# Hybrid gMLP and dilated-attention trunk: ScalarE and VectorE of the attention held to program order, softening one half slot behind the scores, output weights asked for earlier

## The chip, the cores and the metric

The kernel runs on one core of a Trainium2 chip. The metric is device time in microseconds. Engines are named as in the profile: PE (TensorE), DVE (VectorE), ACT (ScalarE), POOL (GpSimd), and SP, which issues most DMAs.

## The reference

Two layers, each a token mixer and a squared-ReLU MLP, with adaLN modulation and a DeepNorm residual; S = 1024, D = 1024. Layer 0 mixes with a chunked causal gMLP, layer 1 with causal dilated attention: three patterns of 16 heads, E = 64, merged by their log-sum-exp.

```python
for g, (window, dilation) in enumerate(B_PATTERNS):    # (128, 1), (512, 4), (2048, 16)
    o, lse = dilated_branch(qkv[:, :, g, 0], qkv[:, :, g, 1], qkv[:, :, g, 2], window, dilation, slopes)
    outs.append(o)
    lses.append(lse)
wts = jax.nn.softmax(jnp.stack(lses, axis=0), axis=0)[..., None]
o = jnp.sum(wts * jnp.stack(outs, axis=0), axis=0)
return o.reshape(B, S, B_HEADS * B_HEAD_DIM) @ w_out
```

## The kernel before

Every fp32 operand is cut into two halves, hi and lo, so that a product is three matmuls (hi hi, hi lo, lo hi). `split` (L100) does it: ACT casts hi (L102), DVE subtracts to lo (L103).

The stages run one after another: adaLN vectors, mixer of layer 0, MLP, the values of layer 1 (`values`, psv on PE; their halves qs are stored by POOL, L1270), the attention (`attention`, L1348), its output projection, the last MLP. The change is in the attention.

The attention works through 24 groups: eight pairs of heads (hp), and for each the patterns g = 2, 1, 0. A group has eight slots of two halves, so a pair has 48 half slots. Functions are hung into half slots with a rank, `in_half(half_slot, rank)` or `at(slot, half)`, and a loop calls those of each half slot in the order of their ranks. These steps make up a group:

- `scores` (rank 1): for two heads, PE multiplies queries and keys into sc, one PSUM bank a head, two in all.
- `soften` (rank 3): DVE adds the bias and takes the minimum (L1551, a custom operation and the reading of its accumulator, stat), ACT takes the exponential and its sum (L1553).
- `transposes` (rank 0) and `halve` (rank 2): PE transposes the probabilities into pT, a split makes pThi and pTlo.
- `weighted` (rank 0, PE, pv L1611), `gather` (ACT copies pv into oT, L1619) and `join` (DVE adds a later part to it, L1623).

Between them `project` streams the projections of queries and keys of later groups (psq and psk, L1434, 512 columns each). Its weights are loaded by SP and cut to wqk_hi and wqk_lo; five units of eight steps run before the first slot.

The three patterns of a pair are merged while the next pair runs (`merge`). `read` loads the minima and sums (mst); `factors` works out three weights per head (mm, ma L1683 to 1687, the exponential L1688 on ACT, mal and ma again L1690 to 1695) and stores them to w_dram (SP, L1697); `spread` loads each back as a row for all partitions (bc, L1704); twelve steps scale (L1716) and add (L1720) and cut the result. The merges of the seventh and eighth pair end in oTs, the operand of the output projection. `load_unit` (L1764) loads that projection's weights (wo) into the buffers that projection weights and others leave; `accumulate` multiplies (psoa, psob L1794), and ACT copies out the first sums (acc, L1803).

The Python order is not the order of the instructions: the tile framework's scheduler puts each engine's instructions in an order of its own. `tc.keep_in_program_order(ins)` pins an instruction behind the one that was issued ahead of it on its engine. Before, only some steps of the merge are pinned.

## Time and profile before

| | us |
|---|---|
| median of three runs | 2736.19 |
| lowest, highest | 2726.71, 2740.26 |
| the profiled execution | 2735.97 |
| its span | 2734.3 |
| attention, first psq to last sc | 1455.8 to 2019.5 |
| mean granted clock of PE | 0.992 |

A row of a timeline has the start, the duration, the engine, the line, the operation, the written and read tiles (buffer numbers left out), the shapes, and in brackets how long the engine had been idle and what it waited for. Matmul rows overlap: the next one's start tells the pace. A row of waits has the engine, its instruction, the releaser, and the total, the number and the longest of such waits.

### The profile page before, as it was taken

To read this page: it belongs to the slowest core of one execution; us is meant where nothing else is said; L and a number is where in the kernel's file an instruction comes from. 1 tells how busy PE (TensorE), PEld (TensorE's weight loads), DVE (VectorE), ACT (ScalarE), POOL (GpSimd) and SP (SyncE) were. 2 spreads that over 40 slices of the span, in tenths; PEclk is the share of its full clock that TensorE was granted. 3 is DMA by queue.
4 is the path that set the end of the run, shared out by engine and by line. 5 is a ranking of instruction groups with operands and counts; after the bars stand their busy time and mean duration, and the time that the engine had idled before them with its cause. 6 is when DMAs were issued, how large, how long until landed. Compare 5 with 4: busy or idle time off the path is not lost.

```text
span 2734.3 us, 37203 instructions
## 1 busy us (share of the span) xinstructions
PE 2653.9 (97%) x13194; PEld 2190.8 (80%) x13194; DVE 2019.3 (74%) x3652; ACT 1389.6 (51%) x2621; POOL 129.9 (5%) x211
## 2 busy tenths in 40 slices
PE   6999999999999999999999999999999999999998
PEld 5788888887888878888888878888777888878886
DVE  6787698787888878666664677777657966577887
ACT  3354375555443454434344666666655755554332
POOL 1000000000000001111111000000010000000000
PEclk9999999999999999999999999999999999999999
DMA  7534337667967656665646555666883554485562
GB/s 263 155 119 135 116 137 225 228 221 255 336 217 257 225 179 214 235 218 204 227 157 194 140 151 157 168 169 175 245 197 112 192 197 153 150 312 193 169 208 85
DMA packets 342223, 525.76 MB, mean 192 GB/s; under 512 B 52572, under 2 KB 169732, under 8 KB 342036
## 3 DMA queue, kind: packets, MB, share of 16 engines
q1 hardware_dynamic: 323060, 455.21, 52.7%
q0 software_dynamic: 18976, 68.17, 6.8%
q8 instruction: 103, 1.69, 0.3%
q14 instruction: 84, 0.69, 0.1%
HBM read 376.93 MB, written 146.36 MB: 191 GB/s over the span
## 4 chain that ended last, share of the span: by engine, by line
PE 61%; DVE 15%; issue 11%; DMA 7%; ACT 5%; SPq 1%; POOL 1%; DVEq 0%; POOLq 0%; ACTq 0%
PE psv L1323 15%; PE psd L957 12%; PE psua L798 7%; PE psk L1434 5%; PE psuc L798 3%; PE psd_wout L389 3%; DMA adaw<-in_ada_w_dram 3%; PE psu L368 3%; PE pv L1611 2%; PE psv L470 2%; ACT p L1553 2%; PE sc L1532 2%; PE psq L1434 2%; DVE adaacc L128 1%; PE psub L798 1%
## 5 line engine op out<-in xcount | busy, mean ns | idle before, releaser
L798 PE MATMUL psua<-right,left 128*128 128x512 f32 x1536 | 363.2, 390 | 0.1
L957 PE MATMUL psd<-rhi,lhi 128*128 128x512 f32 x896 | 349.9, 390 | 3.0 <-ACT part L829 3.0
L957 PE MATMUL psd<-rlo,lhi 128*128 128x512 f32 x896 | 349.4, 390 | 0.2
L957 PE MATMUL psd<-rhi,llo 128*128 128x512 f32 x896 | 349.3, 390 | 0.0
L798 PEld LDWEIGHTS psua<-right,left 128*128 128x128 f32 x1536 | 287.2, 188 | 61.1 <-DVE right L103 1.2
L1553 ACT ACTIVATE p<-p,stat 128x128 f32<-128x128 f32 (+1 forms) x384 | 168.4, 440 | 110.0 <-DVE stat L1551 108.9
L957 PEld LDWEIGHTS psd<-rhi,lhi 128*128 128x128 f32 x896 | 168.6, 188 | 39.0 <-ACT part L829 3.9
L957 PEld LDWEIGHTS psd<-rlo,lhi 128*128 128x128 f32 x896 | 168.7, 188 | 36.0 <-DVE rlo L103 1.1
L957 PEld LDWEIGHTS psd<-rhi,llo 128*128 128x128 f32 x896 | 168.5, 188 | 34.9
L798 PE MATMUL psuc<-right,left 128*128 128x512 f32 x768 | 187.2, 390 | 0.0
L128 DVE SCALAR_TENSOR_TENSOR adaacc<-adaw,silu_c,adaacc 128x512 f32<-128x512 f32 x168 | 128.6, 775 | 55.2 <-DMA adaw<-in_ada_w_dram 54.4
L798 PEld LDWEIGHTS psuc<-right,left 128*128 128x128 f32 x768 | 143.6, 188 | 29.9 <-DVE right L103 0.2
L103 DVE TENSOR_TENSOR pTlo<-pT,pThi 128x512 fp32r<-128x512 f32 (+1 forms) x160 | 98.7, 621 | 63.3 <-ACT pThi L102 62.3
L103 DVE TENSOR_TENSOR left<-ws,left 128x512 fp32r<-128x512 f32 x128 | 87.9, 688 | 74.0 <-ACT left L102 72.2
L103 DVE TENSOR_TENSOR llo<-lraw,lhi 128x1024 fp32r<-128x1024 f32 x112 | 136.4, 1218 | 1.5 <-ACT lhi L102 1.5
L1434 PE MATMUL psk<-form_L,wqk_hi 128*128 128x512 f32 x384 | 131.3, 423 | 0.0
L102 ACT CAST left<-ws 128x512 fp32r<-128x512 f32 x128 | 79.1, 620 | 99.3 <-DVE ws L719 89.5
L102 ACT CAST lhi<-lraw 128x1024 fp32r<-128x1024 f32 x112 | 117.3, 1047 | 9.7 <-PE psd L957 3.3
L1323 PE MATMUL psv<-vrhi,form_S 128*128 128x512 f32 x384 | 120.1, 391 | 1.1 <-DVE vpart L1263 0.6
L1323 PE MATMUL psv<-form_S,vrhi 128*128 128x512 f32 x384 | 118.2, 389 | 0.0
L1551 DVE CUSTOM_DVE_ANT_0 p<-sc,bias 128x128 f32<-128x128 f32 (+1 forms) x384 | 110.4, 346 | 3.5 <-PE sc L1532 3.2
L102 ACT CAST rhi<-rraw 128x1024 fp32r<-128x1024 f32 x48 | 50.5, 1053 | 118.2 <-issue 80.1
(335 smaller groups left out, 6161.4 us busy)
## 6 DMA issues: line engine op xcount, KB each, us to landing
lraw<-forms SPq DMA_DIRECT2D x112, 512.0 KB
adaw<-in_ada_w_dram SPq DMA_DIRECT2D x192, 256.0 KB
up<-in_mlp_w_up_dram SPq DMA_DIRECT2D x64, 512.0 KB
forms<-s SPq DMA_DIRECT2D x128, 256.0 KB
rraw<-in_mlp_w_down_dram SPq DMA_DIRECT2D x64, 512.0 KB
vraw<-in_b_w_qkv_dram SPq DMA_DIRECT2D x50, 512.0 KB
forms<-part SPq DMA_DIRECT2D x96, 256.0 KB
v<-vs POOLq DMA_DIRECT2D x48, 512.0 KB, 4.4
```

What stands on the lines that cost most here:

```text
L102: first = A.copy(hi, src) if hi_engine is A else hi_engine.tensor_copy(hi, src)
L103: return first, lo_engine.tensor_tensor(lo, src, hi, op=ALU.subtract)
L128: ins = V.scalar_tensor_tensor(acc[:], raw[:], silu_c[:, k : k + 1], acc[:], ALU.mult, ALU.add)
L368: T.matmul(dst, s[a], m[b], start=(n == 0), stop=(n == last))
L389: T.matmul(p[:], stat[a][:, k, o : o + P], u[b][:, w], start=n == 0, stop=n == count - 1)
L470: T.matmul(sums[u, half][:], units[u][a_][:, k * P : (k + 1) * P], hT[half][b_][:, k, :], start=k == 0 and a_ + b_ == 0, stop=k == KD - 1 ...
L798: T.matmul(acc, w[:, a, k, :], right[p][:, b, k, :], start=p in (1, 2, 5) and k + a + b == 0, stop=k == 3 and a == 1, skip_group_check=True)
L957: ins = T.matmul(sums[kind, m][:], l[a][:, k, m * P : (m + 1) * P], r[b][:, k, :], start=p in (1, 5, 2, 3) and kp + k + a + b == 0, stop=k ...
L1323: T.matmul(acc, rows[:, m * P : (m + 1) * P], cols_, start=p in (1, 2, 5) and kp + k + a + b == 0, stop=kp == 1 and k == 1 and a == 1, ski ...
L1434: T.matmul(p[:], wu[a][:, k * P : (k + 1) * P], h_op(k, half, b), start=k + c_ == 0, stop=k == KD - 1 and c_ == 2)
L1551: V.tensor_tensor_reduce(out=pr, in0=banks[e][:, sl], in1=st["bias"][:, width - w :], scale=-0.125, scalar=3e38, op0=ALU.add, op1=ALU.min, ...
L1553: A.activation(pr, pr, AF.Exp, bias=nm, scale=-1.0, accum_out=l)
```

## The change

From the lead of the projections to the last slot, every instruction of DVE and ACT is pinned to program order, so that the order in which the loop calls the functions is the order on these two engines; PE, POOL and SP are left to the scheduler. The single pins in the merge go. The half slots are set anew for this: the minimum and the exponential of a score are called one half slot later, as two functions (rank 2.2 and 3); the subtraction of pTlo is a function of its own (rank 2.4), behind the cast of pThi (2) and the joins (2.3); the split of a projection is left to the end of its half slot; the merge's factors come in two parts, a slot and a half apart, and its scaling and adding have other half slots; the last group's scores start in the half slots of the others. Output weights are asked for earlier in program order. The set of instructions is the same on every engine.

```diff
@@ -38,7 +38,22 @@
-    V, A, G, T = nc.vector, nc.scalar, nc.gpsimd, nc.tensor
+    in_order = [False]
+    class Ordered:
+        def __init__(self, engine):
+            self.engine = engine
+        def __getattr__(self, name):
+            call = getattr(self.engine, name)
+            def traced(*a, **k):
+                ins = call(*a, **k)
+                return tc.keep_in_program_order(ins) if in_order[0] else ins
+            return traced
+    V, A, G, T = Ordered(nc.vector), Ordered(nc.scalar), nc.gpsimd, nc.tensor
@@ -1396,6 +1411,12 @@
             def h_op(k, half, part):
...
+            late = []
+            def leave():
+                while late:
+                    late.pop(0)()
@@ -1435,7 +1456,7 @@
-                            split(hi, lo, by_pos(p[:], g))
+                            late.append(lambda hi=hi, lo=lo, p=p, g=g: split(hi, lo, by_pos(p[:], g)))
@@ -1481,7 +1502,7 @@
-                starts = {0: (0, 4, 6, 10) if last_one else (0, 4, 8, 11), 1: (0, 4, 10), 2: (0, 8)}[g]
+                starts = {0: (0, 4, 8, 11), 1: (0, 4, 10), 2: (0, 8)}[g]
@@ -1537,26 +1558,33 @@
                 def soften(m, part):
...
-                    for t, w, sl in spans[part : part + 1]:
-                        for e, st in enumerate(heads):
-                            if w == P and st.get("half") is not None:
-                                pr = st.pop("half")[:, P : 2 * P]
-                            else:
-                                whole = ql.tile([P, 2 * P], F32, name=f"p_{2 * hp + e}_{g}_{t}", tag="p", bufs=16)
-                                pr = whole[:, 0:w]
-                                if w == P and g:
-                                    st["half"] = whole
-                            col = (t % 2) * 4 + t // 2 if g == 1 else t
-                            nm, l = stat[:, 0, e, col : col + 1], stat[:, 1, e, col : col + 1]
-                            V.tensor_tensor_reduce(out=pr, in0=banks[e][:, sl], in1=st["bias"][:, width - w :], scale=-0.125,
-                                                   scalar=3e38, op0=ALU.add, op1=ALU.min, accum_out=nm)
-                            A.activation(pr, pr, AF.Exp, bias=nm, scale=-1.0, accum_out=l)
-                            st["probs"][t] = pr
+                    t, w, sl = spans[part]
+                    for e, st in enumerate(heads):
+                        if w == P and st.get("half") is not None:
+                            pr = st.pop("half")[:, P : 2 * P]
+                        else:
+                            whole = ql.tile([P, 2 * P], F32, name=f"p_{2 * hp + e}_{g}_{t}", tag="p", bufs=16)
+                            pr = whole[:, 0:w]
+                            if w == P and g:
+                                st["half"] = whole
+                        col = (t % 2) * 4 + t // 2 if g == 1 else t
+                        V.tensor_tensor_reduce(out=pr, in0=banks[e][:, sl], in1=st["bias"][:, width - w :], scale=-0.125,
+                                               scalar=3e38, op0=ALU.add, op1=ALU.min, accum_out=stat[:, 0, e, col : col + 1])
+                        st["probs"][t] = pr
+                def exponentials(m, part):
+                    stat = my["stat"]
+                    t, _, _ = my["spans", m][1][part]
+                    col = (t % 2) * 4 + t // 2 if g == 1 else t
+                    for e, st in enumerate(heads):
+                        pr = st["probs"][t]
+                        A.activation(pr, pr, AF.Exp, bias=stat[:, 0, e, col : col + 1], scale=-1.0, accum_out=stat[:, 1, e, col : col + 1])
...
-                        in_half(2 * base + slot + part, 3)(lambda m=m, part=part: soften(m, part))
+                        in_half(2 * base + slot + part + 1, 2.2)(lambda m=m, part=part: soften(m, part))
+                        in_half(2 * base + slot + part + 1, 3)(lambda m=m, part=part: exponentials(m, part))
@@ -1592,7 +1620,12 @@
-                        split(hi[:, 0:end], lo[:, 0:end], pst[:, 0:end])
+                        A.copy(hi[:, 0:end], pst[:, 0:end])
+                        pT[m] = (hi, lo, pst, end)
+                    def low(m, pT=pT):
+                        hi, lo, pst, end = pT[m]
+                        V.tensor_tensor(lo[:, 0:end], pst[:, 0:end], hi[:, 0:end], op=ALU.subtract)
@@ -1631,6 +1664,7 @@
+                        in_half(half_slot, 2.4)(lambda m=m, f=low: f(m))
@@ -1639,7 +1673,7 @@
-                                in_half(when_added, 2)(lambda b=b, f=join: f(b))
+                                in_half(when_added, 2.3)(lambda b=b, f=join: f(b))
@@ -1664,10 +1698,6 @@
-                def in_order(ins):
-                    if hp < N_PAIRS - 1:
-                        tc.keep_in_program_order(ins)
@@ -1675,17 +1705,22 @@
-                @at(*((base + 5, 1) if hp < N_PAIRS - 1 else (base + 1, 1)))
+                @at(*((base + 5, 0) if hp < N_PAIRS - 1 else (base + 1, 1)))
                 def factors():
...
-                    nm, l = st[:, :, 0, :], st[:, :, 1, :]
+                    nm = st[:, :, 0, :]
...
-                    tc.keep_in_program_order(V.tensor_tensor(m[:], nm[:, 0], nm[:, 1], op=ALU.min))
+                    V.tensor_tensor(m[:], nm[:, 0], nm[:, 1], op=ALU.min)
...
+                    box["m"] = a
+                @at(*((base + 6, 1) if hp < N_PAIRS - 1 else (base + 1, 1)))
+                def weights():
+                    l, a = box["st"][:, :, 1, :], box["m"]
@@ -1696,7 +1731,7 @@
-                @at(*((base + 6, 0) if hp < N_PAIRS - 1 else (base + 1, 1)))
+                @at(*((base + 6, 1) if hp < N_PAIRS - 1 else (base + 1, 1)))
@@ -1713,11 +1748,11 @@
-                    in_order(V.tensor_tensor(bc, o, bc, op=ALU.mult))
+                    V.tensor_tensor(bc, o, bc, op=ALU.mult)
...
                 def add(g, half):
...
-                    in_order(V.tensor_tensor(box[0][:, w], box[0][:, w], box[g][:, w], op=ALU.add))
+                    V.tensor_tensor(box[0][:, w], box[0][:, w], box[g][:, w], op=ALU.add)
@@ -1725,7 +1760,7 @@
-                    in_order(split(hi, lo, box[0][:, w])[1])
+                    split(hi, lo, box[0][:, w])
@@ -1736,7 +1771,7 @@
-                    in_half(2 * base + ((23, 25, 29, 31, 35, 37, 39, 41, 43, 45, 47, 51)[n] if hp < N_PAIRS - 2 else n + 22), 4)(f)
+                    in_half(2 * base + ((23, 25, 29, 31, 35, 36, 39, 40, 43, 47, 49, 53)[n] if hp < N_PAIRS - 2 else n + 22), 4)(f)
@@ -1763,7 +1798,7 @@
-            for k, half_slot in ((3, -34), (0, -32), (1, -30), (2, -27), (4, -15), (7, 11), (5, 17), (6, 18)):
+            for k, half_slot in ((0, -64), (1, -56), (3, -48), (2, -38), (4, -33), (7, 11), (5, 17), (6, 18)):
@@ -1832,13 +1867,16 @@
+            in_order[0] = True
...
+                leave()
...
+                    leave()
@@ -1848,7 +1886,8 @@
-            assert next(stream, None) is None
+            assert next(stream, None) is None and not late
+            in_order[0] = False
```

Below, rows of the built programs. In the rows of after every instruction of DVE and ACT has line 51, that of the wrapper. ACT where the values end and the attention begins (qs: high halves of value sums; wqk_hi: of projection weights), before:

```order
L102 CAST wqk_hi<-wq_2_raw 128x1024
L102 CAST wqk_hi<-wk_2_raw 128x1024
L102 CAST qs_1_4_3_11892<-psv_0_1_3_11491 128x512
L102 CAST qs_1_3_0_11909<-vpart_1_6_0_11685 128x512
L102 CAST qs_1_3_1_11926<-vpart_1_6_1_11703 128x512
L102 CAST qs_1_3_2_11943<-vpart_1_6_2_11724 128x512
L102 CAST wqk_hi<-wk_1_raw 128x1024
L102 CAST wqk_hi<-wq_2_raw 128x1024
L102 CAST qs_1_3_3_11960<-vpart_1_6_3_11742 128x512
```

and after:

```order
L51 CAST qs_1_4_3_11892<-psv_0_1_3_11491 128x512
L51 CAST qs_1_3_0_11909<-vpart_1_6_0_11685 128x512
L51 CAST qs_1_3_1_11926<-vpart_1_6_1_11703 128x512
L51 CAST qs_1_3_2_11943<-vpart_1_6_2_11724 128x512
L51 CAST qs_1_3_3_11960<-vpart_1_6_3_11742 128x512
L51 CAST wqk_hi<-wq_2_raw 128x1024
L51 CAST wqk_hi<-wk_2_raw 128x1024
L51 CAST qhi_2_12029<-psq_2_1_12031 128x16x32
L51 CAST qhi_2_12029<-psq_2_0_12058 128x16x32
```

The cuts of the first two projection weights stood ahead of the last five value splits and now stand behind them all.

DVE in the fourth pair's merge (ISA p: softens and their accumulators; mm, ma, mal: factors), before:

```order
L1551 ISA stat_2_15608 128x1
L1683 TENSOR_TENSOR mm_15840<-mst_15705 128x16
L1684 TENSOR_TENSOR mm_15840<-mm_15840,mst_15705 128x16
L1687 TENSOR_TENSOR ma_15843<-mm_15840,mst_15705 128x16 x3
L1690 TENSOR_TENSOR mal_15848<-ma_15843,mst_15705 128x48
L1691 TENSOR_TENSOR mal_15848<-mal_15848 128x16
L1692 TENSOR_TENSOR mal_15848<-mal_15848 128x16
L1623 TENSOR_TENSOR oT_0_15660<-oT_0_15660,pv_0_1_15751 64x512
L1693 RECIPROCAL mal_15848<-mal_15848 128x16
L1695 TENSOR_TENSOR ma_15843<-ma_15843,mal_15848 128x16 x3
L103 TENSOR_TENSOR pTlo_2_0_15868<-pT_2_0_15862,pThi_2_0_15867 128x512
L103 TENSOR_TENSOR qlo_2_15762<-psq_2_1_15763,qhi_2_15761 128x16x32
```

and after:

```order
L51 ISA stat_2_15606 128x1
L51 ISA p_2_6_15838,stat_2_15606<-sc_2_1_15771,bias_2_15607 128x128
L51 ISA stat_2_15606 128x1
L51 ISA p_2_6_15840,stat_2_15606<-sc_2_1_15772,bias_2_15609 128x128
L51 ISA stat_2_15606 128x1
L51 TENSOR_TENSOR pTlo_2_0_15853<-pT_2_0_15847,pThi_2_0_15852 128x512
L51 TENSOR_TENSOR mal_15864<-ma_15826,mst_15697 128x48
L51 TENSOR_TENSOR mal_15864<-mal_15864 128x16 x2
L51 RECIPROCAL mal_15864<-mal_15864 128x16
L51 TENSOR_TENSOR ma_15826<-ma_15826,mal_15864 128x16 x3
L51 TENSOR_TENSOR oT_0_15652<-oT_0_15652,pv_0_1_15749 64x512
```

pTlo of the next group stood behind all the factors and a join; now mm and the first ma are issued ahead of these softens, and pTlo stands right behind the softens, ahead of mal, the reciprocal, the last ma and the join.

DVE in the last merge but one, where bc is scaled for the first time, before:

```order
L1623 TENSOR_TENSOR oT_2_18588<-oT_2_18588,pv_2_1_18629 64x512
L103 TENSOR_TENSOR pTlo_2_0_18666<-pT_2_0_18646,pThi_2_0_18665 128x512
L1716 TENSOR_TENSOR bc_2_18512<-oT_2_17726,bc_2_18512 128x512
L1551 ISA p_1_3_18669,stat_1_18553<-sc_1_1_18651,bias_1_18554 128x256
L1551 ISA stat_1_18553 128x1
L1551 ISA p_1_3_18672,stat_1_18553<-sc_1_1_18652,bias_1_18556 128x256
L1551 ISA stat_1_18553 128x1
```

and after:

```order
L51 ISA p_1_3_18672,stat_1_18557<-sc_1_1_18652,bias_1_18560 128x256
L51 ISA stat_1_18557 128x1
L51 ISA p_1_5_18684,stat_1_18557<-sc_1_1_18651,bias_1_18558 128x256
L51 ISA stat_1_18557 128x1
L51 ISA p_1_5_18686,stat_1_18557<-sc_1_1_18652,bias_1_18560 128x256
L51 ISA stat_1_18557 128x1
L51 TENSOR_TENSOR oT_2_18586<-oT_2_18586,pv_2_1_18625 64x512
L51 TENSOR_TENSOR bc_2_18517<-oT_2_17724,bc_2_18517 128x512 x2
L51 TENSOR_TENSOR pTlo_2_1_18722<-pT_2_1_18716,pThi_2_1_18721 128x512
```

The first scale stood ahead of four softens, and now both of its halves stand behind them and a join, with the next pTlo behind the scale.

## The prediction

> **What bounds the kernel now.** I read the page first, then its busy time in stretches of 100 us, then what PE waited for inside the attention, and last the rows around each of those waits. The page names the engine.
>
> ```profile
> span 2734.3 us, 37203 instructions
> PE 2653.9 (97%) x13194; PEld 2190.8 (80%) x13194; DVE 2019.3 (74%) x3652; ACT 1389.6 (51%) x2621; POOL 129.9 (5%) x211
> ```
>
> PE is busy for 97% of the span, so a reordering on DVE and ACT pays only where PE stands still. The profiled execution took 2735.97 us, 1.7 us more than its span and 0.2 us less than the median of 2736.19 us, so one sum serves for both. Two of the attention's stretches; the columns are the stretch, its length, then the busy share of PE, PEld, DVE, ACT and POOL, and PE's clock.
>
> ```profile
> 1800.00:1900.00 100.00, 98.50 (x708) 83.17 (x707) 78.64 (x251) 69.77 (x215) 4.03 (x9) 1.00 0.61 173
> 1900.00:2000.00 100.00, 92.06 (x635) 77.01 (x634) 69.28 (x224) 61.23 (x195) 6.79 (x12) 0.97 0.82 234
> ```
>
> PE idles 1.5 and 8 us in these 100, and DVE (69 and 79%) and ACT (61 and 70%) have room. Between 1450 and 2040 us these are all of PE's waits: total, times, longest.
>
> ```profile
> PE pv L1611 <- DVE pTlo L103: 11.6, 19, 1.3
> PE psoa L1794 <- ACT acc L1803: 6.4, 1, 6.4
> PE pv L1611 <- ACT pThi L102: 1.8, 5, 0.6
> PE sc L1532 <- DMA bk<-qk: 0.5, 1, 0.5
> PE pv L1611 <- DVE oT L1623: 0.2, 1, 0.2
> ```
>
> They sum to 20.5 us. Idle time can also lower the clock: here stretches of 10 us with their clock, and PE after two waits.
>
> ```profile
> 1560.00:1570.00 10.00, 8.77 (x51) 6.99 (x50) 5.81 (x20) 4.72 (x16) 0.34 (x1) 0.83 0.65 172
> 1580.00:1590.00 10.00, 8.62 (x52) 6.85 (x51) 7.43 (x20) 6.80 (x21) 1.63 (x2) 0.83 0.56 176
> 1630.00:1640.00 10.00, 8.77 (x47) 6.97 (x47) 6.24 (x29) 6.03 (x22) 0.83 (x2) 0.84 0.61 172
> 1700.00:1710.00 10.00, 8.76 (x61) 7.16 (x60) 6.97 (x32) 6.07 (x23) 0.78 (x2) 1.00 0.54 148
> 1980.00:1990.00 10.00, 4.56 (x16) 3.65 (x17) 4.40 (x12) 3.71 (x11) 0.95 (x1) 0.66 1.06 328
> ```
> ```profile
> 1564.20 0.33 PE L1611 MATMUL pv<-pTlo,v 128*128 128x128 f32 x1 [1.23 <-DVE pTlo L103]
> ...
> 1705.44 0.33 PE L1611 MATMUL pv<-pTlo,v 128*128 128x128 f32 x1 [1.24 <-DVE pTlo L103]
> ```
>
> The first three lost 10 x 0.17 or 10 x 0.16, some 1.7 us each, behind a wait of 1.2 to 1.3 us; the fourth, with such a wait too, lost nothing. The last holds the 6.4 us wait; I price its dip like the others. So four dips cost 6.8 us, and **all that the attention can give is 20.5 + 6.8 = 27 us, 1.0% of the run.**
>
> **The merge waits.** Most of the 11.6 us falls once per pair, where the first product of a pattern-2 group meets the factors of the merge. DVE first and PE second, in the fifth pair:
>
> ```profile
> 1769.66 0.21 DVE L1690 TENSOR_TENSOR mal<-ma,mst 128x48 f32<-128x48 f32 x1 [0.95 <-ACT ma L1688]
> ...
> 1771.71 0.69 DVE L103 TENSOR_TENSOR pTlo<-pT,pThi 128x512 fp32r<-128x512 f32 x1
> ```
> ```profile
> 1771.46 0.23 PE L1611 MATMUL pv<-pThi,v 128*128 128x128 f32 x1
> 1772.46 0.33 PE L1611 MATMUL pv<-pTlo,v 128*128 128x128 f32 x1 [0.77 <-DVE pTlo L103]
> ...
> 1838.83 0.33 PE L1611 MATMUL pv<-pTlo,v 128*128 128x128 f32 x1 [0.76 <-DVE pTlo L103]
> ```
>
> DVE runs eight softens in a burst, then the factors, waits 0.95 us for an exponential that stands behind eight others on ACT, and only then cuts pTlo. In the changed order pTlo precedes mal, the reciprocal, the last ma and a join: from 1768.71 (the 0.95 us wait's start) to 1771.71, 3.0 us leave its path. The softens now stand up to a half slot later, and a half slot is 66.4 us (one pair, 1772.46 to 1838.83) over 48, 1.38 us. Net pTlo comes 3.0 - 1.4 = 1.6 us sooner, more than any of these waits. Eight of them are over 0.6 us, one a pair on average (1.23, 1.28, 1.23, 0.89, 1.24, 0.77, 0.76, 0.63), and sum to 8.0 us. Where a weight cut (wqk_lo, 1.2 us, row below) still stands ahead of pTlo, I leave two of 0.9 us. **Term: -8.0 + 1.8 = -6.2 us,** bounds -8.0 and 0, **and three dips, -5.1 us,** bounds -5.1 and 0.
>
> A rule stands against the second part. The Trainium skill, TensorE: Matmul & The Clock Gate, section Why this matters for your kernels, says that the clock falls only after idle gaps of over about 3 us. By it the gaps of 1.2 us cost no clock and the gain would be 5.1 us smaller, some 2732, still inside the forecast's own range below; the rows above disagree (0.83 in the slice of the 1.23 us wait), so I go by them.
>
> **The last merge but one.** One wait holds 6.4 us. SP issues the factors and the six spreads (bc), DVE scales with them, then softens, ACT takes the exponentials and the copy that PE needs.
>
> ```profile
> 1966.63 2.60 SPq L1697 DMA_DIRECT2D w_dram<-ma  x3
> 1969.32 1.19 SPq L1764 DMA_DIRECT2D wo_hi<-wo_parts  x1
> 1974.25 3.70 SPq L1704 DMA_DIRECT2D bc<-w_dram  x6
> ```
> ```profile
> 1981.45 1.02 DVE L1716 TENSOR_TENSOR bc<-oT,bc 128x512 f32<-128x512 f32 x1 [5.68 <-DMA bc<-w_dram]
> ```
> ```profile
> 1982.85 0.51 ACT L1553 ACTIVATE p<-p,stat 128x256 f32<-128x256 f32 x1 [7.80 <-DVE stat L1551]
> ```
> ```profile
> 1965.35 0.33 PE L1611 MATMUL pv<-pThi,v 128*128 128x128 f32 x1
> ...
> 1985.44 0.79 PE L1794 MATMUL psoa<-wo_hi,oTs 128*128 128x512 f32 x1 [6.36 <-ACT acc L1803]
> ...
> 1993.29 0.27 PE L1611 MATMUL pv<-pTlo,v 128*128 128x128 f32 x1
> ```
>
> From the factors' issue to the landing: 1981.45 - 1966.63 = 14.8 us, in which four softens and everything behind them stand still. In the changed order the four softens, a join and a pTlo stand ahead of the scale, so that ACT and PE go on. What waits next is the product at 1993.29, whose pTlo now stands behind two scales: 14.8, plus 2.0 for two scales and 0.7 for pTlo, plus some 2 for two output weight loads that SP now issues ahead of the factors (1.19 us for one), is 19.5 us from 1966.6, or 20.8 from 1965.35. PE's work from 1965.35 to that product is 27.9, less the wait of 6.4 and a dip of 1.7, 19.8 us. So 1.0 us of wait stays. **Term: -5.4 us,** bounds -6.4 and 0, **and half a dip, -0.8.**
>
> **The junction with the values.** What the pinning costs stands at its beginning. ACT, POOL's stores, PE:
>
> ```profile
> 1444.94 1.06 ACT L102 CAST wqk_hi<-wk_raw 128x1024 fp32r<-128x1024 f32 x1
> ...
> 1448.99 0.62 ACT L102 CAST qs<-vpart 128x512 fp32r<-128x512 f32 x1 [2.27 <-DMA qk<-qs]
> 1454.70 0.62 ACT L102 CAST qs<-vpart 128x512 fp32r<-128x512 f32 x1 [5.09 <-DMA qk<-qs]
> ...
> 1462.38 0.62 ACT L102 CAST qs<-vpart 128x512 fp32r<-128x512 f32 x1 [3.13 <-DMA qk<-qs]
> ```
> ```profile
> 1445.08 0.70 POOL L1270 DMA_DIRECT2D qk<-qs  x1 [1.39 <-DVE qs L103]
> 1448.30 0.69 POOL L1270 DMA_DIRECT2D qk<-qs  x1 [2.52 <-DVE qs L103]
> 1450.74 0.69 POOL L1270 DMA_DIRECT2D qk<-qs  x1 [1.75 <-DVE qs L103]
> ```
> ```profile
> 1455.85 0.62 PE L1434 MATMUL psq<-form_L,wqk_hi 128*128 128x512 f32 x2
> ```
> ```profile
> 1444.93 1.23 DVE L103 TENSOR_TENSOR wqk_lo<-wq_raw,wqk_hi 128x1024 fp32r<-128x1024 f32 x1 [0.25 <-PE psv L1323]
> ...
> 1455.97 0.68 DVE L1263 TENSOR_TENSOR vpart<-psv,vpart 128x512 f32<-128x512 f32 x1
> ```
>
> Before, the first two projection weights are cut by 1446 and PE goes from values to projections without a gap. Now these cuts stand behind the last value split, qs, which waits for a buffer that a store has to free. Stores land after 3.9 us (1445.08 to 1448.99) or 6.4 us (1448.30 to 1454.70). With 3.9 the last splits run at 1452.2, 1454.6 and 1457.9 (a store is issued 1.75 us after its split, 1448.99 to 1450.74), the first cut ends at 1459.5, and PE is 3.7 us late, with 0.3 more for the low half, which DVE cuts 1.2 us after the high one. **Term: +4.0 us and a dip, +1.7.** Bounds: 2.5, where no store delays (the last value product's sum, like that at 1455.97, is not there before 1456.7, so the first cut ends at 1458.35 at best), and 8.2, where the last split stays at 1462.38.
>
> **The later softens.** Scores use two PSUM buffers, one a head, so new scores wait until DVE has read the old ones. The softens stand a half slot later; in two places a pair the next scores now follow one half slot behind the last soften (half slots 3 and 4 of a pattern-1 group, 10 and 11 of a pattern-0 group), 16 in all. Queued ahead of a soften on DVE is now, by program order, a pTlo or join that waits for ACT. PE never waited for a soften before, so the rows must be DVE's own waits:
>
> ```profile
> DVE pTlo L103 <- ACT pThi L102: 62.3, 74, 2.9
> ```
>
> Mean 0.84 us. Bounds 0 and 16 x 0.84 = 13.4 us; the soften itself needs four times 0.21 of 1.38 us, so I stay near the lower end: **+3.0 us.** The waits of under 0.6 us (20.5 - 8.0 - 6.4 = 6.1 us) I leave. The output weights cost and bring nothing: no wait of PE above is for them, and their buffers are freed only by the last projections, in either order. The same instructions run on every engine, so no busy time changes.
>
> **Sum:** -6.2 - 5.1 - 5.4 - 0.8 + 5.7 + 3.0 = -8.8 us. 2736 - 9 = **2727 us.**
>
> **The rivals.** (1) *Nearly all waits go:* merges -8.0, dips -5.1 and -1.7, the last merge but one -6.4, half the small waits -3.0, the junction only 2.5 and no dip: -21.7, **2714.** For it: DVE and ACT are idle for a quarter and more. Against: nothing lets ACT run ahead at the junction. (2) *The pinned order is slower:* at each of the 16 tight places scores wait 0.84 us behind a soften that is queued behind an ACT copy, and every second such wait brings a dip: 13.4 + 8 x 1.7 = 27.0, in place of the 3.0 above: +15, **2751.** It decides, against the other terms, once these waits and dips exceed 12 us. For it: 62.3 us of such waits exist on DVE, which were harmless as long as softens could be placed ahead. Against: DVE's share stays below 80%. (3) *It cancels:* the junction takes 8.2 us and two of the merge waits more stay: -8.8 + 4.2 + 1.8 = -3, **2733;** this is also where the change does nothing for the output weights and little else.
>
> **Chances.** Forecast 0.43, (1) 0.21, (2) 0.20, (3) 0.16. What a measurement of this kernel can tell from no change is about 0.5%, 13.7 us: faster means below 2722.5, slower above 2749.9. Faster takes (1) and a fifth of the forecast's spread, 0.29; slower nearly all of (2) and a little of the junction's upper bound, 0.22; the rest is 0.49. The range reaches to (1) and (2): 2711 to 2752; the forecast's own is 2720 to 2736.
>
> **What would show it.** Right: after the last psv, PE waits about 4 us for a wqk cut; no wait of 0.6 us or more for pTlo in most pairs; no clock below 0.9 between 1550 and 1650; the wait of psoa for acc gone, a short one for pTlo in its place; idle in the attention some 15 us. Wrong: a row "PE sc" waiting for a soften with more than some 5 us, a junction over 6 us, or ACT waiting for DVE where PE waits for pThi.

## The result and the profile after

The changed kernel takes 2726.12 us (median of 20 runs, 2712.79 to 2730.65) beside 2736.25 for the kernel before (20 runs, 2726.71 to 2740.26): a ratio of 0.9961, 95% interval 0.9951 to 0.9971, 10 us less. Its profiled execution took 2721.97 us, 4 us under its median, which matters below. The page of after, its span and engines:

```profile
span 2720.3 us, 37241 instructions
...
PE 2653.1 (98%) x13194; PEld 2191.1 (81%) x13194; DVE 2016.9 (74%) x3652; ACT 1394.3 (51%) x2621; POOL 130.5 (5%) x211
```

PE's busy time has hardly moved (2653.9 before). All of PE's waits from 1445 to 2036 us, a stretch that holds the attention of after (total, times, longest):

```profile
PE pv L1644 <- DVE oT L51: 3.2, 7, 1.2
PE psq L1455 <- ACT wqk_hi L51: 2.4, 1, 2.4
PE sc L1553 <- DVE klo L51: 0.9, 1, 0.9
PE sc L1553 <- DMA bk<-qk: 0.6, 1, 0.6
PE pv L1644 <- ACT oT L51: 0.5, 1, 0.5
PE pstat L1684 <- ACT p L51: 0.3, 1, 0.3
PE sc L1553 <- DVE stat L51: 0.2, 1, 0.2
PE pv L1644 <- DVE pTlo L51: 0.2, 1, 0.2
```

20.5 us have become 8.3. The wait for pTlo has gone from 11.6 to 0.2, that of psoa for acc is gone, one for wqk_hi has come. This is the new wait at the junction, its stretch, the stretch that held the first merge's wait before, and one later (length, busy shares of PE, PEld, DVE, ACT, POOL, clock):

```profile
1460.21 1.22 PE L1455 MATMUL psq<-form_L,wqk_hi 128*128 128x512 f32 x2 [2.42 <-ACT wqk_hi L51]
```
```profile
1460.00:1470.00 10.00, 9.79 (x37) 7.96 (x38) 3.14 (x3) 1.69 (x3) 2.30 (x3) 0.83 1.04 284
1560.00:1570.00 10.00, 9.91 (x74) 8.34 (x72) 8.01 (x34) 6.92 (x23) 0.81 (x2) 1.00 0.53 160
1950.00:1960.00 10.00, 9.25 (x55) 7.78 (x55) 7.24 (x35) 7.14 (x24) 0.81 (x2) 0.83 0.86 298
```

Two stretches of the attention still lose 1.7 us to the clock each, where four lost 8.5 us together. The fifth pair's merge, on DVE, ACT and PE:

```profile
1761.47 0.28 DVE L51 CUSTOM_DVE_ANT_0 p<-sc,bias 128x128 f32<-128x128 f32 x1
...
1763.10 0.69 DVE L51 TENSOR_TENSOR pTlo<-pT,pThi 128x512 fp32r<-128x512 f32 x1 [1.33 <-ACT pThi L51]
1763.71 0.20 DVE L51 TENSOR_TENSOR mal<-ma,mst 128x48 f32<-128x48 f32 x1
```
```profile
1761.57 0.39 ACT L51 ACTIVATE p<-p,stat 128x128 f32<-128x128 f32 x1
...
1762.48 0.59 ACT L51 CAST pThi<-pT 128x512 fp32r<-128x512 f32 x1 [0.44 <-PE pT L1612]
1762.96 0.41 ACT L51 ACTIVATE p<-p,stat 128x128 f32<-128x128 f32 x1
```
```profile
1764.32 0.22 PE L1644 MATMUL pv<-pThi,v 128*128 128x128 f32 x1
1764.37 0.27 PE L1644 MATMUL pv<-pTlo,v 128*128 128x128 f32 x1
```

pThi now stands between two pairs of exponentials on ACT, pTlo ahead of mal on DVE; it is there by 1763.8, and PE takes it at 1764.37 without a wait. DVE itself waits more than before, 1.33 us here, and PE doesn't wait for it.

To compare traces I cut them where PE's last value product ends (the start of its last row plus the pace of 0.23 us) and where its last scores start: the attention. Its idle time is the sum of the brackets of PE's rows in it; its clock loss is, over its stretches of 10 us, the length times one minus the clock. The rest is what remains. In a long wait the clock falls before the wait ends, and that part is counted in both columns, which makes the rest too small by 1.9 us in before, 2.8 in e10, 1.5 in e4 and e9, and under 1 us in the others. All in us:

| profile | attention | idle | clock loss | rest |
|---|---|---|---|---|
| before | 563.0 | 19.6 | 8.5 | 534.9 |
| after | 547.8 | 7.4 | 3.4 | 536.9 |
| after, second profile (e10) | 558.7 | 15.7 | 8.5 | 534.4 |
| e1, new places without pins | 577.1 | 23.5 | 11.9 | 541.8 |
| e2, pins in the old places | 584.3 | 21.6 | 18.8 | 543.9 |
| e3, lead freed | 544.2 | 4.9 | 1.7 | 537.6 |
| e4, weights in old places | 554.9 | 12.7 | 6.8 | 535.4 |
| e5, softens early | 565.9 | 13.3 | 5.2 | 547.4 |
| e6, merge in old places | 557.7 | 14.1 | 5.1 | 538.4 |
| e7, scale sooner | 554.6 | 11.7 | 5.1 | 537.8 |
| e8, cuts in two | 545.7 | 7.0 | 3.4 | 535.3 |
| e9, cuts mended | 548.9 | 10.1 | 3.4 | 535.4 |
| e11, DVE alone pinned | 604.2 | 38.1 | 22.1 | 544.1 |
| e12, statistics read behind the blocks | 542.7 | 4.1 | 1.7 | 536.9 |

The first profile of after is 15.2 us shorter in the attention, the second 4.3; the measured 10 us lie between them. What differs between the two is one wait and the clock behind it, which e10 shows. With the double count put back, the rest of before, after, e4, e9, e10 and e12 is 536.8 to 537.2 us; that of e1, e2 and e5 is 542 to 547.

### The profile page after: what moved, and what is told of

Same layout as the page of the kernel before. It is cut to its first block, busy times and chain, and to the rows that moved or that the text cites. A ratio compares the mean times of both kernels' runs of the same rounds, so it can differ in the third digit from the quotient of the medians.

```text
span 2720.3 us, 37241 instructions
## 1 busy us (share of the span) xinstructions
PE 2653.1 (98%) x13194; PEld 2191.1 (81%) x13194; DVE 2016.9 (74%) x3652; ACT 1394.3 (51%) x2621; POOL 130.5 (5%) x211
## 4 chain that ended last, share of the span: by engine, by line
PE 66%; DVE 12%; issue 11%; DMA 6%; ACT 4%; POOL 1%; SPq 0%; DVEq 0%; POOLq 0%; ACTq 0%
PE psv L1338 15%; PE psd L972 11%; PE psua L813 8%; PE psk L1455 5%; PE psuc L813 4%; DMA adaw<-in_ada_w_dram 3%; PE psd_wout L404 3%; PE psq L1455 3%; PE psu L383 3%; PE sc L1553 3%; PE pv L1644 3%; DVE adaacc L51 2%; PE psub L813 2%; PE psv L485 1%; PE pT L1612 1%
## 5 line engine op out<-in xcount | busy, mean ns | idle before, releaser
L51 DVE TENSOR_TENSOR pTlo<-pT,pThi 128x512 fp32r<-128x512 f32 (+1 forms) x160 | 99.5, 622 | 102.4 <-ACT pThi L51 101.0
L51 ACT ACTIVATE part<-part 128x512 f32<-128x512 f32 x224 | 141.4, 632 | 49.8 <-DVE part L51 44.6
L51 ACT CAST lhi<-lraw 128x1024 fp32r<-128x1024 f32 x112 | 117.3, 1047 | 10.5 <-PE psd L972 3.3
L51 ACT CAST pThi<-pT 128x512 fp32r<-128x512 f32 (+1 forms) x160 | 84.6, 529 | 72.8 <-PE pT L1612 57.6
```

The costliest lines, as they stand in the source:

```text
L51: ins = call(*a, **k)
```

## The experiments

Each run was measured beside the kernel before, whose median lay between 2733.3 and 2736.6 us, so ratios can be compared from one run to the next, and single microseconds can't.

**e1 and e2: is it the pins or the places?** Each takes one half of the change. e1 is the changed kernel without the pinning, the merge's single pins back:

```diff
+                    pinned(V.tensor_tensor(bc, o, bc, op=ALU.mult))
...
-            in_order[0] = True
```

> The changed kernel without the pinning: the scheduler orders ScalarE and VectorE by itself again, with the single pins of the merge as before, while all the new half slots stay. My theory (the gain comes from the order that stands on VectorE, not from the half slots as such): the scheduler puts the factors of the merge together again and draws the cuts of the first projection weights ahead of the last value splits, so the junction's 4 us come back as a gain, but waits of TensorE for pTlo return: 2727 to 2736, at most half of the change's gain of 10 us kept. The rival (the half slots do it, the pins are only a means): 2720 to 2726, as fast as the changed kernel or faster by the junction.

Measured: 2745.47 us, ratio 1.0043 (1.0031 to 1.0055). Slower than before, so both texts were too kind: the theory's half of the gain isn't kept, and the rival falls. PE's waits and ACT in the fifth pair:

```profile
PE pv L1644 <- ACT pThi L51: 13.3, 8, 5.0
PE pv L1644 <- DVE pTlo L51: 8.4, 20, 0.7
```
```profile
1770.37 0.41 ACT L51 ACTIVATE p<-p,stat 128x128 f32<-128x128 f32 x1 [1.57 <-DVE stat L51]
...
1773.09 0.39 ACT L51 ACTIVATE p<-p,stat 128x128 f32<-128x128 f32 x1
1773.59 0.58 ACT L51 COPY oT<-pv 64x512 f32<-64x512 f32 x1
1774.19 0.58 ACT L51 CAST pThi<-pT 128x512 fp32r<-128x512 f32 x1
```

Left to the scheduler, the eight softens stand in one burst again, later by a half slot, and so do the eight exponentials; pThi, which PE needs, stands behind all of them. Six of the eight waits for pThi are of this kind, 1.3 to 1.4 us each; the longest, 5.0 us, falls in the last merge but one.

e2 is the kernel before with the wrapper of the change and nothing else of it:

```diff
+    V, A, G, T = Ordered(nc.vector), Ordered(nc.scalar), nc.gpsimd, nc.tensor
...
+            in_order[0] = True
...
+            in_order[0] = False
```

> The kernel before with nothing but the pinning: ScalarE and VectorE of the attention in program order, all functions in their old half slots and ranks. My theory: the old places were written for a scheduler that looks ahead; in strict order softens stand directly behind their own products, so VectorE waits for TensorE and TensorE for what is queued behind, and the merge's scales wait for their rows: clearly slower than before, 2745 to 2790. The rival (pinning alone brings the gain): 2722 to 2732.

Measured: 2755.86 us, ratio 1.0082 (1.0069 to 1.0095), as the theory expected.

```profile
PE pv L1626 <- DVE oT L51: 6.8, 11, 1.4
PE sc L1547 <- DVE stat L51: 6.1, 6, 2.1
```

Here scores do wait for softens, 6.1 us. Its idle time is only 2 us above that of before; 10.3 us are clock and 9.0 the rest (7.1 without the double count in before). Neither half is worth anything alone: beside the kernel before (2734.14 here) one loses 11, the other 22 us, and together they gain 10.

**e5: the softens' place.** The changed kernel, softens and exponentials without their added half slot:

```diff
-                        in_half(2 * base + slot + part + 1, 2.2)(lambda m=m, part=part: soften(m, part))
-                        in_half(2 * base + slot + part + 1, 3)(lambda m=m, part=part: exponentials(m, part))
+                        in_half(2 * base + slot + part, 2.2)(lambda m=m, part=part: soften(m, part))
+                        in_half(2 * base + slot + part, 3)(lambda m=m, part=part: exponentials(m, part))
```

> The changed kernel with softens and exponentials called in the half slot of their own scores again, everything else as changed. The prediction priced the later softens at a loss of 3 us; if that holds, this is 0 to 3 us faster than the changed kernel, 2723 to 2726. The rival, which the trace of after suggests (one wait of 0.2 us of scores for a soften in the whole attention): in strict order an early soften makes VectorE wait for TensorE, and the joins and pTlo queued behind it come late, so the softens' new place is worth most of the pinning: 8 to 25 us slower, 2734 to 2751, with more VectorE waits for sc.

Measured: 2737.4 us, ratio 1.0009 (0.9996 to 1.0021): the whole gain is gone, and the prediction's price for the later softens had the wrong sign. DVE's wait for scores points to the reason:

```profile
DVE p L51 <- PE sc L1553: 48.8, 29, 4.7
```

It was 3.2 us before and 0.7 in after. In strict order a soften that waits for its scores holds up every join and pTlo behind it. Of its 18.1 us over the first profile of after only 5.9 are idle time; 10.5 are the rest, PE's rows that follow one another more slowly: the start-to-start times of the score rows sum to 84.4 us beside 79.7, of pv to 88.7 beside 85.0, of pT to 60.0 beside 57.6.

**e11: one engine alone.** The changed kernel, ACT left to the scheduler:

```diff
-    V, A, G, T = Ordered(nc.vector), Ordered(nc.scalar), nc.gpsimd, nc.tensor
+    V, A, G, T = Ordered(nc.vector), nc.scalar, nc.gpsimd, nc.tensor
```

> The changed kernel with VectorE alone pinned; ScalarE is left to the scheduler. My theory (what counts is the order on VectorE, and ScalarE must follow it): nearly all of the gain stays, and the first weight cuts may run ahead on ScalarE while VectorE's low halves still stand last: 2722 to 2730. The rival (ScalarE's casts of pThi queued behind exponentials are what TensorE waits for, as in the run without pins): waits for pThi of 5 to 13 us return, 2732 to 2742.

Measured: 2776.23 us, ratio 1.015 (1.0135 to 1.0166), worse than either text. PE's longest wait and DVE's:

```profile
PE pv L1644 <- ACT pThi L1623: 19.7, 10, 3.2
```
```profile
DVE pTlo L51 <- ACT pThi L1623: 174.5, 110, 5.9
```

DVE in strict order stands still for 174.5 us behind casts that ACT's own order has put late (101.0 in after). So DVE's order alone doesn't do it. That both engines must follow the same order is a reading of this: ACT pinned alone was not run.

**e3: the junction.** The pins begin behind the lead of the projections:

```diff
-            in_order[0] = True
             for n in range(lead):
...
             due = 0
+            in_order[0] = True
```

> The changed kernel with the pinning begun only after the lead of the projections, so that the first weight cuts can run ahead of the last value splits. My theory: the changed kernel's first projection waits 2.4 us for wqk_hi and then runs some 3 us at half clock, 1.7 us; both go: 4 us faster than the changed kernel, 2720 to 2724. The rival (the wait only moves, to the last value splits that come later and to what they hold up): no difference, 2725 to 2728.

Measured: 2720.56 us, ratio 0.9953 (0.9938 to 0.9968). The wait for wqk_hi is gone from PE's waits, and the attention is 544.2 us, 3.6 shorter than in the first profile of after: 2.5 of idle time and 1.7 of clock less, 0.7 of the rest more. The profile bears the theory out; the two intervals overlap, so the times alone don't.

**e4: the output weights.** Their old half slots in the changed kernel:

```diff
-            for k, half_slot in ((0, -64), (1, -56), (3, -48), (2, -38), (4, -33), (7, 11), (5, 17), (6, 18)):
+            for k, half_slot in ((3, -34), (0, -32), (1, -30), (2, -27), (4, -15), (7, 11), (5, 17), (6, 18)):
```

> The changed kernel with the output weights asked for in the old half slots. My theory (their buffers come free no sooner in either order, and no wait of TensorE is for them): the same time as the changed kernel within 2 us, 2724 to 2728. The rival (asking for them sooner is what took the 6.4 us wait of psoa away): 2730 to 2734.

Measured: 2726.61 us, ratio 0.9973 (0.9961 to 0.9986). The wait of psoa stays away, so the rival falls. Its profile has a wait of 5.1 us for bk, but so has the changed kernel at times (e10): no difference is shown, up to some 0.2%.

**e6 and e7: the two places where the prediction had put the gain.** e6 puts the merge back, e7 puts the scaling of the seventh pair's merge two half slots sooner:

```diff
-                @at(*((base + 5, 0) if hp < N_PAIRS - 1 else (base + 1, 1)))
+                @at(*((base + 5, 1) if hp < N_PAIRS - 1 else (base + 1, 1)))
                 def factors():
...
-                @at(*((base + 6, 1) if hp < N_PAIRS - 1 else (base + 1, 1)))
+                @at(*((base + 5, 1) if hp < N_PAIRS - 1 else (base + 1, 1)))
                 def weights():
...
-                @at(*((base + 6, 1) if hp < N_PAIRS - 1 else (base + 1, 1)))
+                @at(*((base + 6, 0) if hp < N_PAIRS - 1 else (base + 1, 1)))
                 def spread():
...
-                    in_half(2 * base + ((23, 25, 29, 31, 35, 36, 39, 40, 43, 47, 49, 53)[n] if hp < N_PAIRS - 2 else n + 22), 4)(f)
+                    in_half(2 * base + ((23, 25, 29, 31, 35, 37, 39, 41, 43, 45, 47, 51)[n] if hp < N_PAIRS - 2 else n + 22), 4)(f)
```
```diff
-                    in_half(2 * base + ((23, 25, 29, 31, 35, 36, 39, 40, 43, 47, 49, 53)[n] if hp < N_PAIRS - 2 else n + 22), 4)(f)
+                    in_half(2 * base + ((23, 25, 29, 31, 35, 36, 39, 40, 43, 47, 49, 53)[n] if hp < N_PAIRS - 2 else n + 20), 4)(f)
```

> The changed kernel with the merge in its old places: all factors together in one half slot, the spread a half slot before the new one, scales, adds and cuts in the old twelve half slots. My theory (taking mal, reciprocal, ma and a join from ahead of pTlo is what removed the eight waits of 8.0 us and their dips): the pTlo waits return in part, 4 to 10 us slower than the changed kernel, 2730 to 2736. The rival (pinned, the places of the merge do not matter since softens are spread): within 2 us of the changed kernel.

> The changed kernel with the scaling of the seventh pair's merge two half slots sooner, ahead of four softens again as in the kernel before. My theory (this order alone made the 6.4 us wait of psoa): VectorE waits some 3 us longer for bc with the softens behind it, and TensorE waits 2 to 5 us for acc, plus a dip of 1.7: 3 to 6 us slower than the changed kernel, 2729 to 2732. The rival (the wait went because the weights or the rows came sooner): no difference, 2725 to 2728.

Measured: e6 2725.7 us, ratio 0.9969 (0.9959 to 0.998); e7 2724.64 us, ratio 0.9965 (0.9952 to 0.9978). Neither is slower than the changed kernel (0.9961) by more than the intervals' width: in time the rivals held, and both sizes were expected too large. The waits do come back in part, though. PE's wait in e6 and in e7:

```profile
PE pv L1644 <- DVE pTlo L51: 2.6, 5, 0.7
```
```profile
PE psoa L1829 <- ACT acc L51: 4.5, 1, 4.5
```

With all factors ahead of pTlo, the first three merges wait 0.7 us each (1.2 before), the next two not at all (0.8 before), and no dip follows. So the merge's new place took away about half of a wait, in three merges; the rest went, as far as e1 and e6 tell, because the pins split the burst of softens and exponentials (e1 has it whole). In e7 scales ahead of the softens bring 4.5 us of psoa's 6.4 back, which neither profile of the changed kernel has. Its attention is 6.8 us longer than in the first profile of after, but shorter than in the second (e10), and the median doesn't show it.

**e10: the changed kernel again.**

> The changed kernel once more, unchanged, for a second profile of it and for a time beside the other runs. If the trace of after is typical: attention 548 us from the last value product to the last scores, idle 7 to 8 us, no wait of over 1 us for bk, and a ratio of 0.995 to 0.997. The rival, that loads on the queue of SyncE land by chance and the waits of 4.7 to 5.1 us for bk (seen in two experiments) belong to the changed kernel as well: idle 12 to 13 us and 554 us, with the same ratio.

Measured: 2720.29 us (11 runs, 2715.33 to 2731.84), ratio 0.996 (0.9946 to 0.9974). The profiled execution took 2729.68 us, 9 us above that median. PE in the last group, PE's wait, SyncE's queue (SPq) and its longest wait:

```profile
2005.60 1.65 PE L1553 MATMUL sc<-bk,bq 64*128 64x256 f32 x12 [8.92 <-DMA bk<-qk]
```
```profile
1985.52 1.29 SPq L1689 DMA_DIRECT2D st_dram<-stat  x1
1994.41 0.36 SPq L1705 DMA_DIRECT2D mst<-st_dram  x1
1994.86 0.57 SPq L1520 DMA_DIRECT2D bq<-qk  x1
1995.52 1.03 SPq L1520 DMA_DIRECT2D bk<-qk  x1
```
```profile
SPq L1705 <- DMA st_dram<-stat: 17.2, 3, 9.6
```

The rival holds in kind, with sizes larger than it named. PE's other waits are as in the first profile, but the last group's scores wait 8.9 us for a block of keys, where they didn't wait at all in the first profile (its 0.6 us for bk falls at 1667.69). SyncE issues the block's load at 1995.52, behind reads of the last pair's statistics that wait 9.6 and 7.5 us for their stores to land. In the first profile the load was issued at 1992.68:

```profile
1992.68 0.56 SPq L1520 DMA_DIRECT2D bk<-qk  x1
```

Counted from the start of each attention that is 541.4 us in e10 and 535.1 in the first profile, and scores needed the block at 542.5 in both (2000.18 in the first). In e10 it also landed late, 9.9 us behind its issue (6.5 in before, 7.8 in e9); why is not shown. The kernel before has the same queue (15.8 us of such waits from 1960 to 2020) and waits only 0.48 us for this block, with PE 13 us later there. Where this wait shows, it is the change's new bound, and a likely reason, shown in two profiles only, why its runs spread over 18 us (those of before over 14).

**e8, e9, e12: further.** e8 takes e3 and cuts the merge's last step in two, ACT's cast in its place, DVE's subtraction later, since in after DVE waits twelve times for that cast and the join behind it costs PE 1.23 us at 1950:

```diff
-                    split(hi, lo, box[0][:, w])
+                    A.copy(hi, box[0][:, w])
...
+                for half in range(2):
+                    in_half(2 * base + ((48, 54)[half] if hp < N_PAIRS - 2 else 33 + half), 4)(lambda half=half: cut_low(0, half))
```

> The changed kernel with the pins begun after the lead, and the merge's last cuts in two: ScalarE's cast where it stood, VectorE's subtraction one half slot later. In the changed kernel VectorE waits twelve times 1.2 us for that cast, and one join queued behind costs TensorE 1.23 us and a dip, another 0.65. My theory: these go, 2 to 4 us faster than with the freed lead alone (2720.6): 2716 to 2719. The rival (TensorE has slack there and the waits only move): 2719 to 2722.

In e8 the first half's subtraction stands ahead of its cast, so that this half's lo is worked out from an older hi; the amount of work is the same. Measured: 2716.96 us, ratio 0.9925 (0.9908 to 0.9942). The waits for the join fall to 1.2 us, but PE waits once for a pTlo behind the scales of the seventh pair, as DVE stands 10.1 us for their rows:

```profile
PE pv L1644 <- DVE pTlo L51: 5.1, 2, 4.9
```

e9 mends the half slots and puts that merge two half slots later:

```diff
-                    in_half(2 * base + ((48, 54)[half] if hp < N_PAIRS - 2 else 33 + half), 4)(lambda half=half: cut_low(0, half))
+                    in_half(2 * base + ((50, 54)[half] if hp < N_PAIRS - 2 else 35 + half), 4)(lambda half=half: cut_low(0, half))
...
-                    in_half(2 * base + ((23, 25, 29, 31, 35, 36, 39, 40, 43, 47, 49, 53)[n] if hp < N_PAIRS - 2 else n + 22), 4)(f)
+                    in_half(2 * base + ((23, 25, 29, 31, 35, 36, 39, 40, 43, 47, 49, 53)[n] if hp < N_PAIRS - 2 else n + 24), 4)(f)
```

> The freed lead and the cuts in two with the subtractions in their right half slots (each one half slot behind its cast), and the seventh pair's merge two half slots later, since the run with the cuts in two waited 4.9 us for a pTlo behind bc there. My theory: in the attention only waits of some 3 us stay, 15 to 20 us under the kernel before: 2713 to 2719 beside a before of 2733 to 2736. The rival (the rows of bc land later still and the waits move with them, or the time outside the attention grows): 2719 to 2723, no better than the freed lead alone.

Measured: 2718.97 us, ratio 0.9953 (0.994 to 0.9966), just inside the theory's range, though its premise failed: besides the short waits its profile has the one for bk:

```profile
PE sc L1553 <- DMA bk<-qk: 6.1, 1, 6.1
```

e12 is e9 with two of the last pair's reads behind the block loads:

```diff
-                @at(*((base + 1, 1) if hp < N_PAIRS - 1 else (base - 1, 0)))
-                def read():
+                def read(gs):
...
+                        if hp == N_PAIRS - 1:
+                            tc.keep_in_program_order(ins)
...
+                    at(base - 4, 0)(lambda: read((2, 1)))
+                    at(base - 1, 0)(lambda: read((0,)))
```

> The kernel with the freed lead and the mended cuts, with two reads of the last pair's statistics (mst) moved behind the last two block loads (bq, bk) on SyncE's queue. In the second profile of the changed kernel TensorE waits 8.9 us for bk, in the run with the mended cuts 6.1; there the loads stand behind a read that waits 9.6 to 9.8 us for its store to land. My theory (that queue is the new limit, and whether it shows is a matter of some us of landing time): the wait goes, no dip behind it, attention 538 to 543 us in place of 549: 2709 to 2714 beside a before of 2734, and less spread between runs. The rival (the loads themselves land late, or the sixth of the wait moves to the merge at the end): 2717 to 2721.

Measured: 2715.18 us, ratio 0.9923 (0.9906 to 0.994), one us above the theory's range. Its interval lies below that of the change and just touches that of e9; of the kernels that work out every half from its own cast it is the fastest here. SyncE's queue and all of PE's waits over 0.3 us in the attention:

```profile
1981.56 0.56 SPq L1520 DMA_DIRECT2D bk<-qk  x1
...
1988.33 0.60 SPq L1520 DMA_DIRECT2D bk<-qk  x1
1989.03 1.10 SPq L1705 DMA_DIRECT2D mst<-st_dram  x2
```
```profile
PE pv L1644 <- DVE oT L51: 2.5, 7, 0.7
PE sc L1553 <- DVE klo L51: 0.9, 1, 0.9
PE pv L1644 <- ACT oT L51: 0.5, 1, 0.5
PE pv L1644 <- DVE pTlo L51: 0.4, 2, 0.2
```

The load is issued 14 us sooner than in e10, the wait for bk is gone, and the attention is 542.7 us, inside the 538 to 543 expected. That the runs spread less isn't shown: six of e12 lie within 10.8 us, five of e9 within 6.0, eleven of e10 within 16.5.

## Why the prediction was right, and which of its terms were not

The forecast was 2727 us, 9 less; measured were 2726 and 10 less. The step that bounded everything held: PE's busy time stayed, and what was won is idle time and clock in the attention. Term by term:

- **The merge waits, -6.2 and three dips.** All eight waits that the term counts (8.0 us) are gone, and the three dips, so the term was a little small. Its reason was half right. Only five of the eight stand behind the merge's factors. Those of 1.28 us (1584.43) and 0.89 us (1655.09) stand behind a projection's low half and a weight cut, which the change now calls behind pTlo, so the 1.8 us left for weight cuts went too; the one of 0.63 us is for pThi. DVE before, and then after, with wqk_lo at 1582.84:

```profile
1581.83 1.23 DVE L103 TENSOR_TENSOR wqk_lo<-wk_raw,wqk_hi 128x1024 fp32r<-128x1024 f32 x1 [0.38 <-PE sc L1532]
...
1583.70 1.15 DVE L103 TENSOR_TENSOR pTlo<-pT,pThi 128x512 fp32r<-128x512 f32 x2
```
```profile
1581.41 0.69 DVE L51 TENSOR_TENSOR pTlo<-pT,pThi 128x512 fp32r<-128x512 f32 x1 [1.32 <-ACT pThi L51]
```

For the five, pTlo's place ahead of mal is the smaller part: e6 gives it up and gets back 0.7 us of wait in three merges, no dip and no longer time. e1, with the new places but without the pins, has waits of 1.3 to 1.4 us for pThi at six merges.
- **The last merge but one, -5.4.** The 6.4 us of psoa went whole; the 1.0 us expected behind the scales didn't come. In e7's profile 4.5 us come back, so the order named is what makes this wait; that it costs time e7's median doesn't show. One reading was off: the softens didn't stand still for the 14.8 us from the factors' issue to the landing, but for the 5.68 us in the bracket of the scale's row.
- **The junction, +4.0 and a dip.** Measured 2.42 and a dip. The stores were not late: in after ACT's last four value splits wait for sums on DVE, about 2 us each, and none for a store, so the lower bound of 2.5 held. e3 takes the wait away.
- **The later softens, +3.0.** This step failed in sign. The wait that it priced, of scores for softens, came to 0.2 us. It did not see that, in strict order, a soften that waits for its scores holds up what is queued behind it; with the pins in place, e5 takes the added half slot away and loses the whole gain.
- **The small waits, left at 6.1.** PE's waits besides the junction sum to 5.9 us, but they are others: the join behind the merge's last cut (1.23 us and a dip), klo.
- **The output weights, nothing.** Not contradicted (e4).
- **What no term had:** the wait of the last group for bk, none in the first profile, 8.9 us and 5.1 us of clock in the second. It takes back a good part of the 15 us that the first profile shows. So the number came out right in part by luck: this loss was missing, the gains were set too small, the costs of the junction and the softens too large, and these errors met.

Read by times alone, what is shown to matter is the pins, the new places as a whole (e1, e2) and, among these, the later softens (e5); the merge's places, where the prediction had put most of the gain, move waits but not the median (e6, e7).

Of the rivals, the slower one priced pinned softens in their new places, and there it didn't come. In the old places the kernel is slower still than it said (+22 in e2), but only 6.1 us are waits of scores for softens. The Trainium skill's rule that the prediction weighed (TensorE: Matmul & The Clock Gate, Why this matters for your kernels), that only gaps of over some 3 us cost clock, is contradicted again: the 2.42 us at the junction cost 1.7 us of clock.

## What to carry to other kernels

A pinned order and the places in it are one change: either alone lost time here, and a price for one of them can't be read from a trace that has neither. In strict order, ask of every instruction not only who waits for it but what stands behind it while it waits. And when an engine gets faster, look at the queue that was hidden behind it: here SyncE's loads of the last group became the limit, and moving two reads behind them went with a ratio of 0.9923 (e12) beside 0.9953 (e9), two intervals that just touch.

## What the hardware showed that was not expected

How much idle time lowers PE's clock is not fixed by the gap alone. From the attention on, over the ten profiles up to e8, and outside the stretch behind the attention where several waits follow one another, PE waited 31 times for between 1.2 and 1.6 us; 15 of these were followed by a stretch at reduced clock, 16 were not. All ten waits of 2.07 to 2.54 us there were followed by one, always of 0.83 over 10 us, but that is no rule either: in e11 waits of 2.14 and 2.16 us (at 1808.18 and 1879.55) were not.

Part of the answer is a fixed step. A reduced stretch runs at half clock (0.50), and in each trace these stretches begin whole multiples of 3.413 us from one another: in after at 1459.94, 1951.46 and 2060.69 us, 144 and 32 steps apart. Here is the same wait of 1.23 us for a join in after and in e3, with two steps of each (the clock is the third number from the right):

```profile
1950.16 0.30 PE L1644 MATMUL pv<-pThi,v 128*128 128x128 f32 x1 [1.23 <-DVE oT L51]
```
```profile
1948.05:1951.46 3.41, 2.18 (x27) 1.76 (x25) 2.34 (x4) 2.17 (x5) 0.00 (x0) 1.00 0.48 168
1951.46:1954.87 3.41, 3.41 (x14) 3.03 (x13) 3.25 (x23) 2.54 (x13) 0.00 (x0) 0.50 0.78 286
```
```profile
1946.40 0.30 PE L1644 MATMUL pv<-pThi,v 128*128 128x128 f32 x1 [1.23 <-DVE oT L51]
```
```profile
1945.53:1948.94 3.41, 2.54 (x24) 2.30 (x25) 2.98 (x13) 1.92 (x8) 0.00 (x0) 1.00 0.77 308
1948.94:1952.36 3.42, 3.42 (x20) 2.73 (x18) 2.50 (x15) 2.83 (x14) 0.81 (x2) 1.00 0.92 281
```

In after, as in e4 and e10, the wait lies whole inside one step, and the next step runs at 0.50. In e3, as in e7, the edge of a step (1945.53) cuts it, into 0.36 and 0.86 us, and no reduced step follows (the next in e3, at 1955.77, stands behind later waits of 0.34 and 0.93 us in one step). Counted over all fourteen profiles from 1440 to 2430 us, behind a step at full clock with under 1.1 us of idle time 3 of 3872 steps were reduced, with 1.1 to 1.9 us 26 of 57, with more all 35. So where a wait falls in these steps can cost or save 1.7 us; what decides between 1.1 and 1.9 us stays open.

And idle time in the profile seems to be a lower bound: e5 and e2 lose 10 and 7 us in rows that count as busy. A likely reason, which no run shows by itself, is that waits of under 0.2 us vanish in the modelled ends of the matmuls.
